# Keys from raw rows with the norm inside their own norm, and TensorE stages of the small work in batches

## The chip, the cores and the metric

The kernel runs on one core of one Trainium2 chip. The metric is the device time of one execution in microseconds (us). A core has TensorE (matrix products, PE in the rows, with its weight loads as PEld), VectorE (DVE), ScalarE (ACT), GpSimd (POOL), and SyncE (SP), which here issues all DMAs.

## What is computed

Two layers of a hybrid trunk over 528 tokens (16 learned ones in front of 512), 1024 wide. Each layer norms its input, projects it once, and feeds two token mixers side by side: a state-space scan over chunks of 128 tokens, and attention over a window of 128 tokens with 16 always visible ones and a sink per head. Both are projected down, gated, added, projected out, and a squared-ReLU feed-forward follows. Cut to what matters here:

```python
for l in range(DEPTH):
    xn = rms_norm(h, norm1_g[l])
    proj = xn @ w_in[l]
    z, xbc, dt_raw, q, k, v, gate_logits = jnp.split(proj, split_at, axis=-1)
    y_ssd = ssd_mixer(z, xbc, dt_raw, ...)
    y_attn = sliding_window_attention(q, k, v, q_norm_g[l], k_norm_g[l], sinks[l])
    g_ssd, g_attn = jnp.split(jax.nn.sigmoid(gate_logits + b_gate[l]), 2, axis=-1)
    merged = g_ssd * (y_ssd @ w_ssd_down[l]) + g_attn * (y_attn @ w_attn_down[l])
    h = h + merged @ w_o[l]
    hn = rms_norm(h, norm2_g[l])
    h = h + jnp.square(jax.nn.relu(hn @ w_mlp_up[l])) @ w_mlp_down[l]

# in the attention, before the scores
q = rotary(rms_norm(q, q_norm_g), pos)
k = rotary(rms_norm(k, k_norm_g), pos)
```

## The kernel before

**Large products.** Activations lie with channels on partitions and tokens along the free axis, eight rows of 128 channels. Every weight matrix is cut into tiles of 1024 x 128. Each float32 operand is split into a high part and a low part that TensorE takes in one pass, so that one product of 1024 x 128 by a span of tokens is 24 matmuls: high by high, high by low and low by high for eight rows. `dense` (line 537) runs one weight tile over its spans of tokens, two of 264 in layer 0 and one of 512 in most of layer 1, and has the result taken out of its PSUM bank. Its argument `by_row` takes the activation rows in the order in which they are made. The order of the tiles is fixed in `layer_order` (line 55): v, two tiles of keys, eight of queries, then eight groups for the scan (six tiles each), with the gates between and behind them, then the down projections and the feed-forward.

**Small work.** The work between the large products (norms, rotary, attention, scan chunks, their tails, the splitting of weights) is written as Python generators. Each `yield` names what the next stage needs: `ps` or `bank` is a PSUM bank, `pe` is TensorE without a new bank, `data`, `after` and `if` are conditions, others are slots of small rings (`po`, the output bank of attention, has one). They stand in six queues, `w, post, misc, tail, chunk, attn`, in that order of preference, with 2, 6, 5, 2, 3 and 3 tasks alive in each.

**The planner.** `Flow` (line 124) keeps a clock for every engine while the program is written out, with costs of its own for each operation; a large product costs n / 2.4 ns, 110 ns for 264 columns. The order that it makes is the order of each engine's instructions. After every second large product `dense` calls `tick` (line 263), which may start stages whose needs are met by TensorE's planned clock: up to 12, but it returns as soon as one of them has moved TensorE's clock, and does nothing while DVE or ScalarE is more than 3500 ns ahead of TensorE. Banks for small work must leave two spare (`SPARED`). Where the program cannot go on without a task it calls `wait_any`, `finish`, `force` or `until`, which run stages with no large products between.

**The start of a layer.** For each row of the input there are the scaled rows `hg` (input times gain, split into high and low parts) and the squares, summed on DVE. The v products (with dt's columns) read `hg` and are scaled by the inverse root afterwards. At `k == KD - 3` (line 871, row 5 of 8) the sums of squares are put on TensorE as twenty one-column matmuls (`rms_tok`, line 606); POOL takes the power, and ten small matmuls spread it over the partitions (`bcast_tok`). Nine tasks `normal_row` (line 759) then make the normed rows `hn` from the input in place, high part by ScalarE, low part by DVE or POOL. The first key tile reads `hn` with `by_row`, so its products follow the rows as they are made. `rope_tile` (line 922) takes a tile of keys or queries out, swaps halves by four DMAs, multiplies by the rotary tables on POOL and DVE, and sums the squares per head on TensorE (ten matmuls of two columns, kept in `rqk`). `head_rms` (line 979) makes the inverse roots. `keys` (line 994) applies them to the keys; for the queries they enter the scores. Two `rope` slots allow two such tiles at a time.

**Attention.** `attention` (line 1040) is one block of 128 queries and four heads: two stages of scores with two banks each, maximum and exponentials, and one to three pieces in which probabilities are transposed, split and multiplied by v. The down projection of attention (`ad`) reads all of it, split by `attn_split` (line 1485).

Of the kernel before, what the change touches and what calls it, by code (L numbers as in the profile page):

```python
# [9 lines left out]
F32 = mybir.dt.float32  # L10
# [3 lines left out]
ALU = mybir.AluOpType  # L14
# [3 lines left out]
P = 128  # L18
D = 1024
KD = D // P  # L20
# [60 lines left out]
class Ring:  # L81


    def __init__(self, n):
        self.free = [0.0] * n
# [38 lines left out]
class Flow:  # L124
# [11 lines left out]
    SPARED = 2  # L136
    WSPARE = 1200.0
    SPARE = 400.0
    WIDTH = dict(w=2, post=6, misc=5, tail=2, chunk=3, attn=3)
    ORDER = ("w", "post", "misc", "tail", "chunk", "attn")  # L140

    def __init__(self, tc):
        self.tc = tc
        self.t = dict.fromkeys(("pe", "v", "s", "g", "sp", "dge", "dma"), 0.0)
        self.prev = {}
        self.rings, self.queues = {}, {}
        self.written, self.read = {}, {}
        self.end = 0.0
        self.last = 0.0
        self.port = {"v": [], "g": []}  # L150


# [108 lines left out]
        return max(self.t["v"], self.t["s"]) - self.t["pe"] > self.AHEAD  # L261

    def tick(self):
        for _ in range(12):
            if self.busy():
                return
            now = self.t["pe"]
            calm = max(self.t["v"], self.t["s"]) - now < self.CALM
            for t, q in self.active():
                if (calm or q is not self.queues["attn"]) and t.at(self) <= now:  # L270
                    self.step(t, q)
                    break
            else:
                return
            if self.t["pe"] > now:
                return

    def wait_any(self):

# [75 lines left out]
def hybrid_trunk_kernel(ctx: ExitStack, tc: tile.TileContext, h0, params, consts, rope, wdt, w, out,  # L355
# [7 lines left out]
    sm = ctx.enter_context(tc.tile_pool(name="sm", bufs=2))  # L363
# [4 lines left out]
    V = Engine(F, "v", nc.vector)  # L368
# [11 lines left out]
    for k in F.ORDER:  # L380
        F.queue(k, F.WIDTH[k])

# [19 lines left out]
    def C(name, rows=P):  # L402
        a, b = CCOL[name]
        return cst[:rows, a:b]
# [31 lines left out]
    def tt_any(out, a, b, op, spare=None):  # L436

        n = Engine.size(out)
        eng = G if max(F.t["g"], F.t["pe"]) + n * 2.09 + 125.0 < max(F.t["v"], F.t["pe"]) + n / 0.96 + (F.SPARE if spare is None else spare) else V
        if eng is V or n < 512:  # L440
# [96 lines left out]
    def dense(spans, tile_, act, evac, after=None, hold=False, by_row=None, late=None, more=(), keep=False):  # L537

        parts = [(tile_, act)] + list(more)
        steps = [(x, k) for ks in (range(KD - 2), range(KD - 2, KD)) for x in range(3) for k in ks]
        late = [late] if late else []
        if by_row:
            steps = [(0, 0)] + [z for k in range(1, KD) for z in ((0, k), (1, k - 1))] + [(1, KD - 1)]
            steps += [(2, k) for k in range(KD)]

        def place():
            if held and F.rings["ps"].at(F.SPARED + 2) == INF:
                leave()  # L550
            return Slot("ps")

        def product(p, ps, a, b, i):
            x, k = steps[i]
            last = p == len(parts) - 1
            if late and last and k >= KD - 2:
                late.pop()()
            whi, wlo = wt[parts[p][0]].slot.parts
            act = parts[p][1]
            mm(ps.t[:, :b - a], (wlo if x == 2 else whi)[:, k, :], (act.lo if x == 1 else act.hi)(k)[:, a:b],  # L560
               start=(p == 0 and i == 0), stop=(last and i == len(steps) - 1))
            if i % 2:
                F.tick()
                if held and all(t.done for t in first):
                    leave()

        def ready(n, ps):
            a, b = spans[n]

            def out_():  # L570
                F.end = 0.0
                evac(ps.t[:, :b - a], a, b, *([ps] if keep else ()))
                if not keep:
                    ps.free()
                if after and n == len(spans) - 1:
                    after()
            held.append(out_)
            if not hold or all(t.done for t in first):
                leave()

        to = []
        if by_row:
            F.finish(wt[tile_])
            to = [place() for _ in spans]
            for i, (x, k) in enumerate(steps):
                if x < 2:
                    F.force(by_row[k + x:k + x + 1])
                for n, (a, b) in enumerate(spans):
                    product(0, to[n], a, b, i)
            wt[tile_].slot.free()  # L590
            for n in range(len(spans)):
                ready(n, to[n])
            return
        for p, (t, _) in enumerate(parts):
            F.finish(wt[t])
            for n, (a, b) in enumerate(spans):
                if p == 0:
                    to.append(place())
                for i in range(len(steps)):
                    product(p, to[n], a, b, i)  # L600
                if n == len(spans) - 1:
                    wt[t].slot.free()
                if p == len(parts) - 1:
                    ready(n, to[n])
# [34 lines left out]
    nrm = {}  # L639
# [61 lines left out]
    hg = Split("hg", KD)  # L701
# [23 lines left out]
    for l in range(depth):  # L725
# [31 lines left out]
        hn = Split("hn", KD)  # L757
# [16 lines left out]
        normal = [F.put("post", normal_row(k)) for k in range(KD + 1)]  # L774
        tables_t = F.put("misc", tables())
# [92 lines left out]

        for k in range(KD + 1):
            F.force(made[k:k + 1])  # L870
            if k == KD - 3:

                F.force(made)
                while not nrm["summed"]:
                    F.step(norm_t[0], F.queues["misc"])
            if k < KD:
                v_row(k, 0, start=k == 0)
            if k:
                v_row(k - 1, 1)
# [20 lines left out]
        for c in range(5):  # L900
            ps = banks[c]
# [17 lines left out]
        kr, kn = kn_u[:, 0:2, :], kn_u[:, 2:4, :]  # L919
        rqk = lay.tile([P, 5, 20], F32, name="rqk", tag="rqk")  # L920

        def rope_tile(kind, spans, m, dst, c_lo):
            slot = Slot("rope")
            j = slot.j
            qx, sq = au[:, j, :T], au[:, 2 + j, :T]
            cosg, sing = table[kind]
            lo = spans[0][0]
            here = []

            def evac(ps, a, b):  # L930
                S.copy(qx[:, a:b], ps)

            def swap():
                here.append(1)

            dense(spans, (l, kind, m), hn, evac, after=swap, by_row=normal if kind == "k" and m == 0 else None)

            def rest():
                yield {"if": lambda: here, "sq": 1}

                t1 = Slot("sq", "t1")
                for o in range(0, P, 32):
                    i = o ^ 32
                    F.dma(t1.t[o:o + 32, lo:T], qx[i:i + 32, lo:T])
                S.activation(out=sq[:, lo:T], in_=qx[:, lo:T], func=AF.Square)
                yield {"after": [tables_t]}
                for x, y in ((lo, 264), (264, T)):
                    G.tensor_tensor(out=dst[:, x:y], in0=qx[:, x:y], in1=cosg[:, x:y], op=ALU.mult)
                yield {"data": lambda: [t1.t[:, lo:T]]}
                tt_any(t1.t[:, lo:T], t1.t[:, lo:T], sing[:, lo:T], ALU.mult)  # L950
                yield {"ps": 1}
                ps = Slot("ps")
                for c in range(c_lo, 5):
                    t0 = CHUNKS[c][0]
                    mm(ps.t[:, 2 * c:2 * c + 2], sq[:, t0:t0 + P], C("blk"))
                slot.free()
                yield

                col = 16 + 2 * m if kind == "k" else 2 * m
                f, e = (1.0 / 64.0, EPS) if kind == "k" else (1.0, 64.0 * EPS)  # L960
                V.tensor_scalar(out=rqk[:, c_lo:, col:col + 2], in0=ps.t[:, 2 * c_lo:10].rearrange("p (c x) -> p c x", x=2),
                                scalar1=f, scalar2=e, op0=ALU.mult, op1=ALU.add)
                ps.free()
                V.tensor_tensor(out=dst[:, lo:T], in0=dst[:, lo:T], in1=t1.t[:, lo:T], op=ALU.add)
                t1.free()
            return F.put("misc", rest())
# [12 lines left out]
        def head_rms(tasks, c0_, h0_, h1_):  # L979

            yield {"after": tasks, "raw": 1}
            tmp = Slot("raw", "rqs")
            t = [tmp.t[:, o:o + 100].rearrange("p (c h) -> p c h", c=5)[:, c0_:, h0_:h1_] for o in (0, 100)]
            v = rqk[:, c0_:, h0_:h1_]
            rsqrt(v, t)
            V.tensor_copy(out=v, in_=t[1])
            tmp.free()

        kt = [rope_tile("k", ALL, m, kr[:, m, :T], 0) for m in range(2)]
# [603 lines left out]
        hg = Split("hg", KD)  # L1593
# [68 lines left out]
        if not last:  # L1662
            hg = hg2
# [106 lines left out]
```

## Time and profile before

| | |
|---|---|
| time, median of 3 runs | 2383.31 us (2380.02 to 2384.53) |
| the profiled execution | 2383.62 us |
| its span, first to last instruction | 2381.5 us |
| mean granted clock of TensorE | 0.991 |
| TensorE busy | 2344.6 us, 98% |
| DVE, ScalarE, POOL busy | 1167.9, 1027.6, 1328.7 us |
| DMA, mean | 108 GB/s |

A row of the timeline gives the start, the time until the last end, the engine, the line, the operation with its tiles, the shapes and a count of merged instructions; in brackets stands idle time before it and what ended it. A matmul's recorded time overlaps that of the next one, so the pace is read from one start to the next. Line 431 is the helper for all matmuls, 434 that for transposes, 348 the wrapper for all other engines, so groups are told apart by their tiles: `hnh` and `hnl` are the parts of the normed rows, `hgh` and `hgl` of the raw scaled rows, `whi` and `wlo` of a weight tile.

### The profile page before, as it was taken

How to read it: one execution, taken by the hardware profiler on the slowest of the kernel's cores; microseconds unless marked ns; L12 is line 12 of the kernel's file. 1: busy time of each engine (PE TensorE's matmuls, PEld its weight loads, DVE VectorE, ACT ScalarE, POOL GpSimd, SP SyncE). 2: the span in 40 equal slices, each digit the busy share in tenths (PEclk: the TensorE clock that was granted, in tenths of full speed). 3: DMA queues.
4: the chain of work that ended last, by engine and by line, in shares of the span. 5: the costliest groups of instructions: out<-in, count | busy, mean ns of one | idle time of the engine just before them, and what ended most of it. 6: DMA issues, size and time to landing. Idle time of an engine off the chain costs nothing.

```text
span 2381.5 us, 41784 instructions
## 1 busy us (share of the span) xinstructions
PE 2344.6 (98%) x16038; PEld 2144.2 (90%) x16038; DVE 1167.9 (49%) x2499; ACT 1027.6 (43%) x2007; POOL 1328.7 (56%) x1751
## 2 busy tenths in 40 slices
PE   7999999999999999999999999999999999999999
PEld 7999999999999999999998888989988788888887
DVE  5577788877412332122146867877773124222121
ACT  5365666555422233232244556656553223333221
POOL 4554555665655555455546554456855655555554
PEclk8999999999999999999999999999999999999999
DMA  4223333443453322222242233334444433222222
GB/s 145 90 86 99 90 100 101 113 102 102 122 184 112 135 81 89 93 94 89 92 153 83 72 115 107 102 98 112 115 121 133 169 117 132 90 96 97 98 91 104
DMA packets 133589, 257.42 MB, mean 108 GB/s; under 512 B 16470, under 2 KB 66318, under 8 KB 133390
## 3 DMA queue, kind: packets, MB, share of 16 engines
q1 hardware_dynamic: 133390, 254.75, 33.9%
q8 instruction: 127, 2.08, 0.3%
q14 instruction: 72, 0.59, 0.1%
HBM read 232.03 MB, written 17.33 MB: 105 GB/s over the span
## 4 chain that ended last, share of the span: by engine, by line
PE 90%; DVE 4%; DMA 2%; ACT 1%; POOL 1%; issue 1%; SPq 0%; POOLq 0%; ACTq 0%; DVEq 0%
PE ps L431 87%; PE ps L434 2%; DMA gm<-ac_dram 2%; DVE at L348 1%; DVE rqs L348 0%; ACT gm L348 0%; DVE xb L348 0%; DVE ar L348 0%; POOL wlo L348 0%; DVE xh L348 0%; DVE h L348 0%; DVE raw L348 0%; ACT whi L348 0%; DVE gm L348 0%; DVE es L348 0%
## 5 line engine op out<-in xcount | busy, mean ns | idle before, releaser
L348 POOL TENSOR_TENSOR wlo<-wraw,whi 128x256 fp32r<-128x256 f32 x1272 | 981.9, 804 | 777.3 <-ACT whi L348 754.3
L348 ACT CAST whi<-wraw 128x1024 fp32r<-128x1024 f32 x340 | 355.5, 1046 | 730.5 <-PE ps L431 698.6
L431 PE MATMUL ps<-hnl,whi 128*128 128x266 f32 (+2 forms) x2048 | 400.7, 311 | 1.7 <-POOL hnl L348 1.5
L431 PE MATMUL ps<-hnh,whi 128*128 128x266 f32 (+2 forms) x2048 | 398.2, 310 | 1.0 <-DVE vm L348 0.6
L431 PE MATMUL ps<-hnh,wlo 128*128 128x266 f32 (+2 forms) x2048 | 393.7, 310 | 0.0
L431 PEld LDWEIGHTS ps<-hnl,whi 128*128 128x128 f32 x2048 | 306.7, 191 | 16.6 <-POOL hnl L348 3.4
L431 PEld LDWEIGHTS ps<-hnh,wlo 128*128 128x128 f32 x2048 | 306.3, 191 | 14.0 <-issue 0.2
L431 PEld LDWEIGHTS ps<-hnh,whi 128*128 128x128 f32 x2048 | 305.1, 190 | 13.8 <-PE ps L431 0.8
L348 DVE SCALAR_TENSOR_TENSOR h<-ps,h 128x264 f32<-128x264 f32 (+1 forms) x120 | 62.2, 518 | 324.3 <-PE ps L431 324.3
L431 PE MATMUL ps<-hgl,whi 128*128 128x264 f32 (+1 forms) x768 | 154.0, 322 | 0.4 <-DVE hgl L348 0.4
L431 PE MATMUL ps<-hgh,wlo 128*128 128x264 f32 (+1 forms) x768 | 153.4, 321 | 0.0
L431 PE MATMUL ps<-hgh,whi 128*128 128x264 f32 (+1 forms) x768 | 153.3, 321 | 0.0
L431 PE MATMUL ps<-hidl,whi 128*128 128x264 f32 (+1 forms) x768 | 152.7, 320 | 0.0
L431 PE MATMUL ps<-hidh,wlo 128*128 128x264 f32 (+1 forms) x768 | 152.6, 320 | 0.0
L431 PE MATMUL ps<-hidh,whi 128*128 128x264 f32 (+1 forms) x768 | 152.5, 320 | 0.0
L348 DVE SCALAR_TENSOR_TENSOR tmp<-ps,rbc 128x264 f32<-128x264 f32 (+1 forms) x96 | 49.5, 515 | 179.0 <-PE ps L431 170.2
L431 PE MATMUL ps<-y,whi 128*128 128x264 f32 (+1 forms) x768 | 137.0, 320 | 0.0
L431 PEld LDWEIGHTS ps<-hgl,whi 128*128 128x128 f32 x768 | 119.3, 189 | 11.5 <-DVE hgl L348 0.6
L431 PEld LDWEIGHTS ps<-hgh,whi 128*128 128x128 f32 x768 | 119.4, 189 | 11.2
L431 PEld LDWEIGHTS ps<-hgh,wlo 128*128 128x128 f32 x768 | 119.1, 189 | 11.0
L431 PEld LDWEIGHTS ps<-hidh,wlo 128*128 128x128 f32 x768 | 118.7, 188 | 11.1
L431 PEld LDWEIGHTS ps<-hidl,whi 128*128 128x128 f32 x768 | 118.7, 188 | 11.0
(213 smaller groups left out, 3892.0 us busy)
## 6 DMA issues: line engine op xcount, KB each, us to landing
wraw<-w_dram SPq DMA_DIRECT2D x344, 512.0 KB, 3.2
gm<-ac_dram SPq DMA_DIRECT2D x64, 256.0 KB, 5.0
et<-ac_dram SPq DMA_DIRECT2D x128, 64.0 KB, 4.6
t<-au SPq DMA_DIRECT2D x48, 66.0 KB, 2.0
h<-h_dram SPq DMA_DIRECT2D x8, 264.0 KB, 5.7
at<-rope_dram SPq DMA_DIRECT2D x4, 528.0 KB, 4.1
y_dram<-xb SPq DMA_DIRECT2D x4, 528.0 KB
yr<-y_dram SPq DMA_DIRECT2D x8, 264.0 KB, 3.1
```

Source lines behind the costliest of these rows:

```text
L348: inst = fn(*a, **k)
L431: F.run("pe", cost, [o], [lhsT, rhs], PE.matmul(out=o, lhsT=lhsT, rhs=rhs, start=start, stop=stop))
L434: F.run("pe", 108.0 if in_.shape[1] > 64 else 60.0, [o], [in_], PE.transpose(out=o, in_=in_, identity=C("ident", k)[:, :k]))
```

## The change

The planner gets a field `GAP` of 3600 ns. In `tick`, stages that need TensorE or a bank are passed over unless that much of TensorE's planned time has gone by since the end of the last batch; other stages go on. In an open tick up to 24 stages may start, and it no longer returns after the first one on TensorE. The key tiles take `hg` in place of `hn`. Their scale is then missing the inverse root r of the token's norm: the head sums are multiplied by r squared (`r2`) before the small constant is added, and the inverse roots of the keys by r. `by_row` goes to the first query tile. The rest of the key work waits for all `normal_row` tasks, since its output lies on the buffer of the input rows. In layer 0 the sums of squares move from row 5 to behind row 7.

```diff
+    GAP = 3600.0
+        self.batch = 0.0

     def tick(self):
-        for _ in range(12):
+        begin = self.t["pe"]
+        open_ = begin - self.batch >= self.GAP
+        for _ in range(24):
             if self.busy():
-                return
+                break
             now = self.t["pe"]
             calm = max(self.t["v"], self.t["s"]) - now < self.CALM
             for t, q in self.active():
+                if not open_ and any(k in ("pe", "ps", "bank") for k in t.needs):
+                    continue
                 if (calm or q is not self.queues["attn"]) and t.at(self) <= now:
                     self.step(t, q)
                     break
             else:
-                return
-            if self.t["pe"] > now:
-                return
+                break
+        if self.t["pe"] > begin:
+            self.batch = self.t["pe"]

-            if k == KD - 3:
+            if k == (KD - 3 if l else KD):

+        r1 = nrm["rt"]
+        r2 = sm.tile([P, 5], F32, name="rt2", tag="rt2")
+        V.tensor_tensor(out=r2, in0=r1, in1=r1, op=ALU.mult)

-            dense(spans, (l, kind, m), hn, evac, after=swap, by_row=normal if kind == "k" and m == 0 else None)
+            dense(spans, (l, kind, m), hg if kind == "k" else hn, evac, after=swap,
+                  by_row=normal if kind == "q" and m == 0 else None)

-                yield {"after": [tables_t]}
+                yield {"after": [tables_t] + (normal if kind == "k" else [])}

-                V.tensor_scalar(out=rqk[:, c_lo:, col:col + 2], in0=ps.t[:, 2 * c_lo:10].rearrange("p (c x) -> p c x", x=2),
-                                scalar1=f, scalar2=e, op0=ALU.mult, op1=ALU.add)
+                o = rqk[:, c_lo:, col:col + 2]
+                x = ps.t[:, 2 * c_lo:10].rearrange("p (c x) -> p c x", x=2)
+                if kind == "k":
+                    V.scalar_tensor_tensor(out=o, in0=x, scalar=f, in1=r2[:, c_lo:, None].broadcast_to([P, 5 - c_lo, 2]),
+                                           op0=ALU.mult, op1=ALU.mult)
+                    V.tensor_scalar(out=o, in0=o, scalar1=e, scalar2=None, op0=ALU.add)
+                else:
+                    V.tensor_scalar(out=o, in0=x, scalar1=f, scalar2=e, op0=ALU.mult, op1=ALU.add)

-            V.tensor_copy(out=v, in_=t[1])
+            if h0_ == 16:
+                V.tensor_tensor(out=v, in0=t[1], in1=r1[:, c0_:, None].broadcast_to([P, 5 - c0_, h1_ - h0_]), op=ALU.mult)
+            else:
+                V.tensor_copy(out=v, in_=t[1])
```

## Rows read from the trace of the kernel before

**Rows 1.** The page, part 1: busy us, share of span, instructions.
```profile
PE 2344.6 (98%) x16038; PEld 2144.2 (90%) x16038; DVE 1167.9 (49%) x2499; ACT 1027.6 (43%) x2007; POOL 1328.7 (56%) x1751
```
**Rows 2.** The page, part 4: the chain that ended last, by line.
```profile
PE ps L431 87%; PE ps L434 2%; DMA gm<-ac_dram 2%; DVE at L348 1%; DVE rqs L348 0%; ACT gm L348 0%; DVE xb L348 0%; DVE ar L348 0%; POOL wlo L348 0%; DVE xh L348 0%; DVE h L348 0%; DVE raw L348 0%; ACT whi L348 0%; DVE gm L348 0%; DVE es L3
```
**Rows 3.** Timeline of PE near 602 us (start, us, engine, operation, count).
```profile
602.00 0.89 PE L431 MATMUL ps<-hnh,wlo 128*128 128x264 f32 x6
602.73 0.41 PE L431 MATMUL ps<-hnh,whi 128*128 128x264 f32 x2
...
603.94 0.49 PE L434 MATMUL ps<-cst,xb 128*128 128x128 f32 x3
604.27 0.39 PE L431 MATMUL ps<-xb 128*128 128x128 f32 x2
604.41 0.49 PE L431 MATMUL ps<-hnh,whi 128*128 128x264 f32 x2
604.74 0.91 PE L431 MATMUL ps<-hnl,whi 128*128 128x264 f32 x6
```
**Rows 4.** Timeline of PE: sums of squares of layer 0, next v products.
```profile
18.41 3.40 PE L431 MATMUL ps<-cst,sq 128*128 128x1 f32 x20 [1.35 <-DVE sq L348]
...
21.67 1.55 PE L431 MATMUL ps<-wvh,hgh 128*128 128x288 f32 x5
```
**Rows 5.** Timeline of DVE and POOL: the root of these sums.
```profile
21.85 0.17 DVE L348 TENSOR_SCALAR rt<-ps 128x5 f32<-128x5 f32 x1 [1.31 <-PE ps L431]
...
22.09 1.18 POOL L348 TENSOR_TENSOR rt<-rt,cst 128x5 f32<-128x5 f32 x1 [11.43 <-DVE na L348]
```
**Rows 6.** Timeline of PE: the two key tiles of layer 0.
```profile
35.19 0.65 PE L431 MATMUL ps<-hnh,whi 128*128 128x264 f32 x4
...
43.24 1.11 PE L431 MATMUL ps<-hnl,whi 128*128 128x264 f32 x2 [0.44 <-POOL hnl L348]
...
47.32 0.90 PE L431 MATMUL ps<-hnh,whi 128*128 128x264 f32 x6
...
53.29 1.06 PE L431 MATMUL ps<-cst,adt 128*32 128x128 f32 x8
```
**Rows 7.** Timeline of PE: the first key tile of layer 1.
```profile
1255.32 0.60 PE L431 MATMUL ps<-hnh,whi 128*128 128x264 f32 x3 [0.59 <-DVE vm L348]
```
**Rows 8.** PE's waits (us, times, longest); uses of `ar` (ns min/median/max).
```profile
PE ps L431 <- DVE ar L348: 5.8, 11, 1.6
PE ps L431 <- POOL rx L348: 3.5, 3, 1.7
...
L348 DVE TENSOR_TENSOR ar<-ps,ar x92: 205/681/693, 120.2 to 1641.1; 128x512 fp32r<-128x512 f32 x56, 32x512 fp32r<-32x512 f32 x32, 16x64 fp32r<-16x64 f32 x4
```
**Rows 9.** Stretches: length, busy (count) of PE, PEld, DVE, ACT, POOL, clock, DMA, GB/s.
```profile
19.60:26.40 6.80, 6.80 (x31) 6.80 (x31) 1.19 (x4) 2.26 (x5) 1.18 (x1) 0.50 0.43 157
...
40.00:46.90 6.90, 6.06 (x24) 4.99 (x23) 6.28 (x17) 2.29 (x7) 3.70 (x6) 0.51 0.23 77
...
84.40:91.20 6.80, 6.80 (x32) 6.80 (x33) 6.45 (x9) 2.58 (x4) 3.21 (x6) 0.50 0.37 117
...
118.50:660.00 541.50, 533.60 (x4343) 508.48 (x4343) 400.88 (x964) 313.86 (x756) 300.07 (x395) 1.00 0.36 102
...
1241.50:1245.00 3.50, 3.50 (x17) 3.50 (x17) 0.17 (x1) 0.79 (x3) 1.17 (x1) 0.51 0.37 139
```
**Rows 10.** Timeline of PE: scores begin, attention ends, `ad` begins, per layer.
```profile
108.23 0.28 PE L431 MATMUL ps<-k2h,q 128*128 128x256 f32 x1
...
447.89 0.63 PE L431 MATMUL ps<-ar,vt 128*128 128x512 f32 x2
...
665.87 0.90 PE L431 MATMUL ps<-ah,whi 128*128 128x264 f32 x6
...
1642.96 0.62 PE L431 MATMUL ps<-ar,vt 128*128 128x512 f32 x2
...
1841.31 1.55 PE L431 MATMUL ps<-ah,whi 128*128 128x512 f32 x6
```

## The prediction

> **What bounds the kernel now.** I read the busy table first: TensorE (PE in the rows) is busy 2344.6 of 2381.5 us [rows 1], so only some 37 us are open idle time, and the reader should expect a change of order to be worth a per cent or two at most. The chain of waits says the same: 87% of it is the large and small matmuls of one helper line [rows 2]. So the time is the sum of what TensorE has to stream, plus its waits, plus the stretches at the lower clock. The other engines matter only where TensorE waits for them or where they set when a buffer comes free.
>
> The large products run at a plain pace: six of 264 columns take 602.00 to 602.73, 0.122 us each [rows 3]. A small matmul between them takes about 0.11 us (603.94 to 604.27 for three transposes). Is a change-over from large to small and back dear? From 603.94 to 604.74 there are five small and two large matmuls in 0.80 us [rows 3]; five at 0.11 and two at 0.122 make 0.79. So a change-over costs about 0.01 us, and **fewer, longer interruptions gain next to nothing by themselves**. What batching can win is waits and clock. Both have prices in the trace: the waits list [rows 8], and four of the stretches at 0.50 to 0.51 of the full clock [rows 9], where a large product takes twice its time, so that a stretch of 6.8 us loses 3.4 and one of 3.4 loses 1.7.
>
> The profiled execution took 2383.62 us, of which 2381.5 are the span; the median of the three runs is 2383.31, so the sum below may be set against 2383.6.
>
> **The change part by part: the start of layer 0.** Before, the sums of squares stand behind the v products of row 4. TensorE waits 1.35 us for the last one, the twenty one-column matmuls end at 21.67, and from 19.6 to 26.4 the clock is at half, 1.2 GHz [rows 4, 9]. After, they stand behind the products of row 7: six more groups of five at 0.13 us (288 columns by the pace above), 4 us, which cover the wait. I take back the wait, 1.35, and the half clock, 3.4 us. New is that only five v products (0.7 us) then stand between the sums and the broadcast that needs their root: DVE takes 0.17 us and POOL 1.18 us for it, until 23.27, and with a hop it is some 1.75 us after the sums [rows 5]. So about 1.1 us of wait appears; it would be nothing if the planner's tick runs the sums a row earlier. Sum: 1.35 + 3.4 - 1.1 = 3.7 us gained, bounds 2 and 5.
>
> Then the first key tile. Before, it reads the normed rows as they are made: from 35.19 to 47.32, 12.1 us, with waits such as 0.44 us for a row from POOL, and the clock at half from 40.0 to 46.9 [rows 6, 9]. The second tile takes 47.32 to 53.29, 6.0 us. With raw rows both inputs are there long before, since the v products have just read them; the first tile then takes 48 x 0.122 = 5.9 us and 6.2 us come back. The wait for rows moves to the first query tile, which starts after two key tiles, 11.7 us later. Its rows were complete by about 43.2 before [rows 6]; after, the key tiles end near 35.2 - 3.7 + 11.7 = 43.2, and the ten tiny matmuls of the first key tile's head sums go ahead of the queries as they did before. The rows start no later, because the v products ahead of the root run at full clock. So I charge 0.5 us, bounds 0 and 2.5. The rest of the key work waits for all the normed rows (its output overlies them); that wait sits in the planner's queue, and behind it on POOL stand the rotary products of the keys and the low parts of weights. The head sums themselves need only ScalarE's square, so TensorE is not held. The added scaling is some six DVE operations on 5 to 10 numbers per partition, 0.17 us each by the nearest row [rows 5], beside TensorE's products: nothing on the path, 1 us if the cover were gone. The squared norm is right by algebra and moves no DMA; the four swaps of each key tile leave SP in the same order behind its copy, some 6 us earlier. Layer 0 in sum: 3.7 + 6.2 - 0.5 = **9.4 us**, bounds 5 and 11.5.
>
> Layer 1 keeps its place of the sums, so its half clock from 1241.5 stays. Its first key tile waits only 0.59 us [rows 7], which goes: **0.6 us**, bounds 0 and 1.
>
> **The batches.** A stage that needs TensorE may now begin only when 3600 ns of planned products have passed since the last batch: at the planner's 110 ns that is 34 large products (it looks after every second one), 34 x 0.122 = 4.15 us plus the batch itself. Steps on DVE, ScalarE and POOL go on in between. A stage that became ready inside the gap has then been ready for up to 4 us, so the plan's small errors no longer show as waits. The waits that belong to such stages are led by 5.8 us for the split probabilities and 3.5 for the key factors [rows 8]; with six smaller ones of that list they are about 18 us. A stage that becomes ready just before its batch still waits, and inside a batch several stages follow each other without products between them. I take half, **9 us**, bounds 2 and 15. For the clock: the stretch from 84.4 [rows 9] follows a wait for the key factors and loses 3.4 us. I take that back, **3 us**, bounds -8 (longer runs of tiny matmuls lower the clock elsewhere) and 8.
>
> The price is latency. Each chain now moves at most one TensorE stage per batch. Attention is the longest: in layer 0 there are 20 tasks (five blocks, four heads of keys), four with one piece, four with two and twelve with three; only one may hold the output bank, and one with n pieces passes n+1 stages there, so 4x2 + 4x3 + 12x4 = 68 stages in a row. Before, scores start at 108.2 and the last value product stands at 447.9: 340 us, 5.0 us per stage. The products that need all of it start at 665.9 [rows 10]. From 108.2 to there stand some 3140 large products, 92 batches of 34, 6.05 us each with the small work. At one stage per batch attention ends at 108 + 68 x 6.05 = 520 us; at 1.35 batches per stage it ends just at 666. Layer 1 has 60 stages and 198 us of slack [rows 10], so it bears about 1.45. Between two stages lie a copy, a subtraction of 0.68 us [rows 8] and the queue of DVE, which is 74% busy from 118.5 to 660 [rows 9], so most steps fit one gap and some need two; I take 1.25, which costs nothing. The last group's chunks must be through at the same point and also pass one gap per stage: I charge **2 us** for both layers as an allowance, bounds 0 and 15 (three batches of some 5 us). The feed-forward half has almost no such stages and stays.
>
> Sum: 2383.6 - 9.4 - 0.6 - 9 - 3 + 2 = 2363.6, say **2363 us**, 0.9% faster.
>
> **The rivals.** First, the keys gain, the batches do not: waits move from single stages to the heads of batches and the clock is as before. Then 2383.6 - 10 = 2373, still faster. For it: TensorE's waits are already short and spread. Against: they come where plan and chip differ by a few tenths, and a gap of 4 us is longer.
>
> Second, on the slow side: **attention is starved**. There are eight banks; a span of large products holds one and often its predecessor's, two are kept spare, the output holds one, and a score stage wants two at once. When a batch gives two to chunks first, scores must wait for the next, since no bank comes free inside a batch. By this mechanism a stage costs 1.6 batches in layer 0: of 92 batches 109 are wanted, 17 are missing, some 11 stages run with no products above them at about 2.5 us each (copy, subtraction, hops, the wait for the next), and the splitting of eight rows of about 1 us follows uncovered: 27 + 8 = 35 us, so 2398. It decides at 1.35 batches per stage. For it: DVE's load, and that attention comes last in the order of the queues. Against: before, the pace was 5.0 us where 558 / 68 = 8.2 are allowed. The Trainium skill ("Trainium Kernel Development and Optimization", Best Practices) names exhausted PSUM as a cause of regular gaps; no run here shows it for this kernel.
>
> Third, **the clock**. It fell at 1241.5 although TensorE was busy in all of that stretch [rows 9], right behind twenty one-column matmuls. Batches put such sums, ten at a time, beside others. Seven more stretches of 6.8 us would take 24 us: 2387. Against: from 118.5 to 660 the clock was 1.00 throughout [rows 9]. The Trainium skill ("TensorE: Matmul & The Clock Gate", HAM oscillation) ties the fall to waits between bursts; by that rule alone bunching would only help, but the trace shows a fall without idle time.
>
> Last, that the change does not do what it says: the query tile inherits the whole wait for the rows and the drop of the clock with it, and nothing is won at the start: 2373.
>
> **How the numbers follow.** The forecast has 0.53, the first rival 0.15, starved attention 0.18, the clock 0.09, the inherited wait 0.05. The forecast's own range is 2350 to 2374. To leave out no more than 2 in 10 the range goes from 2350 to 2397, which takes in most of the starved case. Faster by over 0.2% (4.8 us, about what a measurement of this kernel can tell from no change) is the forecast, nearly all of the first and last rivals: 0.71. Within 0.2% come most of the clock's case and mild starvation: 0.12. Slower: 0.17.
>
> **What would show each step.** The first key tile some 6 us long and starting near 31.5 us, no half clock from 19.6 to 26.4 nor from 40 to 47, and no row waits in the first query tile; runs of small matmuls some 34 products apart; less waiting on the split probabilities and key factors; the last value product of layer 0 between 500 and 650 us, and no idle TensorE before the products that read attention. The prediction is wrong if that point shows attention stages with gaps, if half-clock stretches multiply between 118 and 660, or if the first query tile waits as the first key tile did.

## The result and the profile after

The changed kernel takes 2352.59 us (median; 2351.39 to 2355.22) against 2383.92 for the kernel before on the same chip: a ratio of 0.9877 with a 95% interval of 0.9865 to 0.9889. The forecast was 2363. The profiled execution took 2351.39 us, its span is 2349.5.

The page of the changed kernel, part 1 (busy us, share, count), answers to [rows 1]:

```profile
PE 2322.6 (99%) x16038; PEld 2129.6 (91%) x16038; DVE 1186.7 (51%) x2511; ACT 1027.7 (44%) x2007; POOL 1327.6 (57%) x1733
```

TensorE runs the same 16038 matmuls and is busy 22 us less: what was saved is mostly time in which it counted as busy. Lines 439, 442 and 356 are here what 431, 434 and 348 were before; the numbers differ from version to version. TensorE's waits (total us, times, longest) answer to [rows 8]:

```profile
PE ps L439 <- ACT wvh L356: 9.5, 1, 9.5
PE ps L439 <- DVE q L356: 5.2, 2, 4.6
PE ps L439 <- DVE ar L356: 2.2, 3, 0.8
...
PE ps L439 <- POOL rx L356: 0.5, 1, 0.5
```

The first line is the wait for the first weights, which every version has. The split probabilities `ar` fell from 5.8 to 2.2 us, the key factors `rx` from 3.5 to 0.5. A new one of 4.6 us stands before the first scores. Four stretches (columns as in [rows 9]):

```profile
19.60:26.40 6.80, 6.06 (x49) 5.80 (x49) 2.16 (x6) 2.53 (x5) 1.18 (x1) 1.00 0.46 157
40.00:46.90 6.90, 6.90 (x60) 6.90 (x59) 6.11 (x11) 3.65 (x9) 6.62 (x9) 1.00 0.59 179
...
94.40:101.20 6.80, 4.59 (x21) 4.62 (x22) 3.95 (x19) 1.97 (x4) 2.06 (x4) 0.50 0.04 10
...
835.10:841.90 6.80, 6.80 (x33) 6.80 (x33) 0.17 (x1) 0.32 (x1) 1.18 (x1) 0.50 0.22 77
```

The clock is whole where [rows 9] had it at half (19.6, 40.0), and the last two lines are all the half clock that is left between the first rise of the clock and the last matmul: 13.7 us, where the kernel before had 41 in eight stretches.

The timeline of TensorE at the start of layer 0 answers to [rows 4, 6]:

```profile
20.90 2.29 PE L439 MATMUL ps<-cst,sq 128*128 128x1 f32 x20
23.05 0.91 PE L439 MATMUL ps<-wvh,hgl 128*128 128x288 f32 x5
24.70 1.48 PE L439 MATMUL ps<-cst,rt 16*128 16x16 f32 x10 [0.74 <-POOL rt L356]
25.93 5.49 PE L439 MATMUL ps<-wvl,hgh 128*128 128x288 f32 x40
31.26 0.89 PE L439 MATMUL ps<-hgh,whi 128*128 128x264 f32 x6
...
33.70 0.51 PE L439 MATMUL ps<-hgh,wlo 128*128 128x264 f32 x2 [0.34 <-POOL wlo L356]
...
37.66 0.90 PE L439 MATMUL ps<-hgh,whi 128*128 128x264 f32 x6
...
44.58 0.73 PE L439 MATMUL ps<-hnh,whi 128*128 128x264 f32 x4
```

The sums have no wait, the broadcast of the root waits 0.74 us, the first key tile takes 6.4 us from 31.26, and the first query tile, which begins at 44.58, runs through the normed rows without a wait. Attention, for [rows 10]: the last value product of layer 0 and the first product that reads attention:

```profile
577.87 0.70 PE L439 MATMUL ps<-ar,vt 128*128 128x512 f32 x2
...
642.10 0.89 PE L439 MATMUL ps<-ah,whi 128*128 128x264 f32 x6
```

**Where the time went.** Every large product has the same number in both kernels, so the time between two of them can be compared. "Waits" is TensorE's idle time there, "clock" half of the time in which it was busy in half-clock stretches (a wait in such a stretch counts as a wait alone), "rest" what is left; gains in us.

| Large products | before | after | gain | waits | clock | rest |
|---|---|---|---|---|---|---|
| 0 to 120, v | 25.99 | 21.80 | 4.2 | 0.6 | 3.4 | 0.2 |
| to 216, two key tiles | 20.23 | 13.31 | 6.9 | 1.7 | 3.0 | 2.2 |
| to 600, queries, first scores | 76.55 | 74.07 | 2.5 | -1.2 | 4.5 | -0.9 |
| to 3672, rest of attention's half | 533.90 | 523.45 | 10.5 | 6.5 | 0 | 3.9 |
| to 8280, feed-forward half | 567.49 | 569.01 | -1.5 | 0 | -1.7 | 0.2 |
| to 11500, the same half of layer 1 | 726.42 | 716.72 | 9.7 | 2.6 | 5.1 | 2.0 |
| to the end | 417.52 | 417.51 | 0 | 0 | 0 | 0 |

In sum 32 us: 10 of waits, 14 of clock, 8 that fall under neither.

### The profile page after: what moved, and what is told of

Read it like the earlier page. It is cut to its first block, busy times and chain, and to the rows that moved or that the text cites. A ratio compares the mean times of both kernels' runs of the same rounds, so it can differ in the third digit from the quotient of the medians.

```text
span 2349.5 us, 41761 instructions
## 1 busy us (share of the span) xinstructions
PE 2322.6 (99%) x16038; PEld 2129.6 (91%) x16038; DVE 1186.7 (51%) x2511; ACT 1027.7 (44%) x2007; POOL 1327.6 (57%) x1733
## 4 chain that ended last, share of the span: by engine, by line
PE 92%; DVE 4%; ACT 1%; POOL 1%; issue 1%; DMA 1%; SPq 0%; ACTq 0%; DVEq 0%; POOLq 0%
PE ps L439 90%; PE ps L442 3%; DVE rqs L356 1%; DVE at L356 1%; DVE xh L356 0%; POOL wlo L356 0%; DVE xb L356 0%; DMA gm<-ac_dram 0%; ACT gm L356 0%; ACT whi L356 0%; DVE raw L356 0%; DVE ar L356 0%; DVE gm L356 0%; DVE qa L356 0%; SPq L232 0%
## 5 line engine op out<-in xcount | busy, mean ns | idle before, releaser
L439 PE MATMUL ps<-hnh,whi 128*128 128x266 f32 (+2 forms) x1984 | 371.7, 305 | 0.0
L439 PE MATMUL ps<-hnl,whi 128*128 128x266 f32 (+2 forms) x1984 | 369.5, 305 | 0.0
L439 PE MATMUL ps<-hnh,wlo 128*128 128x266 f32 (+2 forms) x1984 | 365.6, 304 | 0.0
L439 PEld LDWEIGHTS ps<-hnl,whi 128*128 128x128 f32 x1984 | 293.0, 189 | 13.4
L439 PEld LDWEIGHTS ps<-hnh,wlo 128*128 128x128 f32 x1984 | 291.6, 189 | 13.2
L439 PEld LDWEIGHTS ps<-hnh,whi 128*128 128x128 f32 x1984 | 292.0, 189 | 12.6 <-issue 0.3
L439 PE MATMUL ps<-hgh,wlo 128*128 128x264 f32 (+1 forms) x832 | 165.0, 320 | 0.3 <-POOL wlo L356 0.3
L439 PE MATMUL ps<-hgl,whi 128*128 128x264 f32 (+1 forms) x832 | 164.5, 319 | 0.4 <-DVE hgl L356 0.4
L439 PE MATMUL ps<-hgh,whi 128*128 128x264 f32 (+1 forms) x832 | 164.1, 319 | 0.0
L439 PEld LDWEIGHTS ps<-hgh,wlo 128*128 128x128 f32 x832 | 128.6, 190 | 11.5 <-POOL wlo L356 0.5
L439 PEld LDWEIGHTS ps<-hidl,whi 128*128 128x128 f32 x768 | 118.8, 188 | 11.1
L439 PEld LDWEIGHTS ps<-hidh,wlo 128*128 128x128 f32 x768 | 118.7, 188 | 11.1
```

Of the source, the lines that this page charges most:

```text
L439: F.run("pe", cost, [o], [lhsT, rhs], PE.matmul(out=o, lhsT=lhsT, rhs=rhs, start=start, stop=stop))
```

## The experiments

Two theories stood against each other for the batches. **Time in hand**: a stage that begins some microseconds after the plan calls it ready doesn't show the plan's errors as waits, and no half clock follows them. **Change-overs**: each turn from large to small matmuls costs by itself, and fewer turns gain. The kernel before plans a stage on TensorE 0.1 us behind the step before it (`LATP = 100.0`), so the gap between batches is one way to give a stage time, a larger `LATP` is another.

All twelve in one table with the kernels before and after, each ratio against executions of the kernel before in the same round (medians 2381.96 to 2383.92 us). The balance is that of the profiled execution, from the first matmul to the last; the first 3 to 6 us, ahead of the clock's first rise, are at half clock too and stand in the rest. "Turns" is the count of runs of small matmuls, "last value" the end of the last value product of layer 0.

| Kernel | median us | ratio to before, 95% | turns | waits | clock | rest | last value |
|---|---|---|---|---|---|---|---|
| before | 2383.92 | | 484 | 23.9 | 20.1 | 2324.5 | 448 |
| after | 2352.59 | 0.9865 to 0.9889 | 220 | 13.7 | 5.7 | 2316.8 | 579 |
| keys_only | 2378.68 | 0.9970 to 0.9989 | 489 | 22.0 | 20.9 | 2321.7 | 472 |
| batches_3200 | 2370.10 | 0.9921 to 0.9958 | 230 | 18.5 | 16.1 | 2321.1 | 582 |
| both_3200 | 2360.75 | 0.9892 to 0.9922 | 227 | 16.5 | 9.1 | 2317.8 | 581 |
| spread_3200 | 2376.50 | 0.9968 to 0.9987 | 485 | 20.9 | 15.1 | 2319.8 | 645 |
| gap_0 | 2401.79 | 1.0056 to 1.0100 | 355 | 38.1 | 25.6 | 2323.0 | 429 |
| gap_1800 | 2372.27 | 0.9941 to 0.9979 | 291 | 24.0 | 11.8 | 2319.3 | 506 |
| margin | 2362.91 | 0.9895 to 0.9934 | 482 | 16.8 | 16.8 | 2316.1 | 603 |
| sums_early | 2356.88 | 0.9872 to 0.9906 | 221 | 14.3 | 11.1 | 2317.1 | 582 |
| margin_1000 | 2350.34 | 0.9851 to 0.9884 | 483 | 8.4 | 10.0 | 2318.2 | 518 |
| b1800_l1500 | 2353.73 | 0.9864 to 0.9893 | 298 | 11.0 | 12.7 | 2316.5 | 562 |
| cost_550 | 2391.26 | 1.0022 to 1.0048 | 211 | 39.9 | 19.7 | 2318.4 | 655 |
| margin_1000_cost | 2373.69 | 0.9948 to 0.9978 | 490 | 26.5 | 14.3 | 2318.7 | 524 |

The rest lies between 2316 and 2323 us for all the changed versions, and doesn't go with the turns: the lowest, margin, has 482, the highest, gap_0, 355. What tells them apart is mostly the waits and the clock, which together run from 18 to 64 us.

**keys_only**: the change with the old tick.

```diff
-        for _ in range(24):
+        for _ in range(12):
...
-                if not open_ and any(k in ("pe", "ps", "bank") for k in t.needs):
-                    continue
...
+            if self.t["pe"] > now:
+                return
```

> Keys from raw rows and the later sums, with the planner's old tick (one TensorE stage per tick, no gap). Theory, margin: the keys gain 10 us at the start of layer 0 and 0.6 in layer 1, the rest of the gain belongs to the batches: 2373 us, bounds 2368 and 2377; the first key tile takes 6 us, the half-clock stretches at 19.6 and 40 us are gone, those further on remain in number. Rival, all from the keys: the batches only look as if they gained, because the keys shift the rest: 2355 us.

It took 2378.68 us, less than half of the gain that was expected. The start did gain: the first query tile ends 11.0 us earlier, counted from the first matmul. But from product 8280 to 11500 it lost 8.6 us (735.00 against 726.42), with waits of 12.0 where there were 8.3 and a clock loss of 10.2 where there were 5.1. TensorE's order there is another one than in the kernel before, again with stages 0.1 us behind the plan; that the earlier start throws the order, and that the order makes the waits, is my reading and was not tested. And of the half clock at the start, which was to be gone, 6.8 us stand at 24.6.

**batches_3200 and both_3200**: the new tick with a gap of 3200 ns on the kernel before (old keys, old place of the sums), and the whole change with that gap.

```diff
-    GAP = 3600.0
+    GAP = 3200.0
```

> The kernel before with the new tick and a gap of 3200 ns of planned products, keys from normed rows. Theory, margin: the batches gain what the keys do not, some 20 us: 2363 us, bounds 2358 and 2370, with PE's waits on split probabilities below 3 us and fewer half-clock stretches after 60 us. Rival, all from the keys: 2384. The start of layer 0 stays as before, with a first key tile of 12 us.

> The changed kernel with a gap of 3200 instead of 3600 ns, the control for the two runs that use 3200. All theories: 2353 us, bounds 2349 and 2357; some 240 runs of small matmuls.

2370.10 and 2360.75: the batches give some 13 us without the new keys, the keys another 9 with the batches. The second lies above what was expected, the first just past its upper bound: with 400 ns less between batches the gain is smaller (both_3200 against the changed kernel: 0.9907 and 0.9877, with intervals that don't meet).

**gap_0 and gap_1800**: the whole change with gaps of 0 and of 1800 ns; the first edit is

```diff
-    GAP = 3600.0
+    GAP = 0.0
```

> The changed kernel with a gap of 0: a tick may set up to 24 stages at once, but none is held back. Theory, margin: without the gap no stage has time in hand, so the waits on late inputs come back as in the kernel before: 2371 us, bounds 2366 and 2376. Rival, many stages per tick are what counts: 2355.

> The changed kernel with half the gap, 1800 ns. Theory, margin: half the time in hand covers more than half of the small errors of the plan: 2358 us, bounds 2353 and 2364. Rival, change-overs: the gain of the batches goes with the number of runs of small matmuls, which rises to some 330: 2362.

Both theories missed both runs. gap_1800, at 2372.27, lies 8 us above the upper bound of the first and 10 above the figure of the second, with 291 turns. gap_0, at 2401.79, is slower than the kernel before, though it has 355 turns where that has 484. An open tick at gap 0 starts all stages that are ready, each as soon as the plan allows, with no large products between. Its waits, first four lines, and one of them in the timeline:

```profile
PE ps L439 <- POOL xdd L356: 10.8, 5, 3.0
PE ps L439 <- DVE ar L356: 9.8, 12, 4.5
PE ps L439 <- ACT wvh L356: 9.2, 1, 9.2
PE ps L439 <- DVE q L356: 5.0, 2, 4.5
```

```profile
315.33 0.50 PE L439 MATMUL ps<-ar,vm 128*128 128x512 f32 x1 [0.71 <-DVE ar L356]
```

`ar` alone is 9.8 us in 12 waits, [rows 8] had 5.8 in 11. So grouping without distance did harm here. Its waits are 38.1 us in sum; with the gap they fall to 24.0 (1800), 16.5 (3200) and 13.7 us (3600), and the time with them. Fewer turns gained nothing.

**spread_3200**: gap 3200, but the stages that a batch would hold start one in each tick, with two large products between.

```diff
-        open_ = begin - self.batch >= self.GAP
+        open_ = self.left or begin - self.batch >= self.GAP
...
+            if self.t["pe"] > begin:
+                break
...
         if self.t["pe"] > begin:
+            self.left = True
             self.batch = self.t["pe"]
+        else:
+            self.left = False
```

> As the control with a gap of 3200, but the stages of a batch are set one per tick with two large products between, until none is ready; so stages have waited as long as in the control, while the small work interrupts the products about twice as often (some 450 runs of small matmuls). Theory, margin: a change-over costs 0.01 us, so within 4 us of the control. Rival, change-overs: bunching itself is the gain, some 0.08 us for each of 220 more interruptions: 15 to 20 us slower than the control.

It took 2376.50, 16 us more than both_3200, which is the number of the change-over theory, and by time alone that theory would stand. The balance says otherwise: with 485 turns in place of 227 its rest is 2.0 us larger, 0.008 us for each turn more, where 16 us would be 0.06. The loss has a place. From product 3672 to 4056, the first that read attention, it took 62.9 us where both_3200 took 46.7:

```profile
644.40 0.63 PE L444 MATMUL ps<-ar,vt 128*128 128x512 f32 x2
...
647.09 0.41 PE L444 MATMUL ps<-ah,whi 128*128 128x264 f32 x2
649.29 0.92 PE L444 MATMUL ps<-ah,whi 128*128 128x264 f32 x2 [1.79 <-ACT ah L361]
652.17 1.12 PE L444 MATMUL ps<-ah,whi 128*128 128x264 f32 x2 [1.96 <-ACT ah L361]
...
657.54 0.81 PE L444 MATMUL ps<-al,whi 128*128 128x264 f32 x2 [2.91 <-POOL al L361]
...
661.32 1.17 PE L444 MATMUL ps<-cst,zs 128*128 128x1 f32 x4 [1.66 <-DVE zs L361]
```

```profile
650.40:667.50 17.10, 10.35 (x39) 8.96 (x40) 10.27 (x17) 7.92 (x16) 14.20 (x22) 0.50 0.43 141
```

The last value product stands at 644.40, the products that read it begin at 647.09. TensorE waits 8.9 us there for the split of the rows and the last chunks, and the clock is at half for 17.1 us. That is the starved attention of the prediction's second rival: 68 stages in 541 us are 8.0 us each. Outside this place spread_3200 is some 4 us faster than both_3200 in the two profiles; its profile is the fastest of its ten executions, 5.6 us below their median, so a part of the 16 us has no place.

**margin**: keys_only with 2.0 us in hand for each stage on TensorE, no batches.

```diff
-    LATP = 100.0
+    LATP = 2000.0
```

> Keys from raw rows with the planner's old tick, and LATP raised from 100 to 2000 ns: a TensorE stage counts as ready 2 us after its inputs by the plan, and there is no gap and no batch. Theory, margin: time in hand is what gains, so most of the batches' gain comes without batches: 2358 us, bounds 2353 and 2365, with some 450 runs of small matmuls. Rival, change-overs: no batches, no gain over keys alone: 2373.

2362.91, within what the theory allowed, with 482 turns. Of the 26 us between keys_only and the changed kernel it brings 16 with no batch at all. And it loses some that it need not: two rows of its timeline among the products that read attention, where the tails of the last chunks are late.

```profile
641.90 0.58 PE L433 MATMUL ps<-cst,zs 128*128 128x1 f32 x4 [0.91 <-DVE zs L350]
646.85 1.32 PE L433 MATMUL ps<-cst,rg 128*128 128x128 f32 x4 [4.37 <-POOL rg L350]
```

With a half clock behind them this place costs 9.3 us (56.0 against 46.7). Another 6.9 go in layer 1, where products 8280 to 11500 take 724.21 us and in margin_1000, the next run, 717.32. Two microseconds for each stage were too much here.

**margin_1000**: the same with 1.0 us.

> The new keys without batches, each stage on TensorE planned 1.0 us behind the step before it, where 0.1 us was planned and 2.0 us in the run margin. The theory, that time in hand is what the batches give: most single waits of the kernel without it were under 1.7 us, so 1.0 us catches the larger part, and attention is no longer late at the products that read it, where 2.0 us cost 5.3 us of waits and 3.4 of clock: 2362 us (2356 to 2368), some 480 runs of small matmuls. The rival, that only distances of several microseconds between stages help: 2372.

2350.34 us (2348.41 to 2355.34), a ratio of 0.9868: below what was expected, and not to be told from the changed kernel, with 483 turns and no batches. Its waits, the first three lines:

```profile
PE ps L433 <- ACT wvh L350: 9.3, 1, 9.3
PE ps L433 <- DVE mx L350: 2.8, 2, 1.8
PE ps L433 <- ACT whi L350: 0.8, 1, 0.8
```

`ar` and `rx` are gone. So one number in the planner gives the whole gain without a batch, and attention ends at 518 rather than 579. That time in hand is also what the batches give is the reading that fits the four gaps, whose waits fall as the gap grows. It is not proof: each version is one order, and two below have time in hand and are 23 and 39 us slower.

**b1800_l1500**: batches 1800 ns apart and 1.5 us in hand.

```diff
-    LATP = 100.0
+    LATP = 1500.0
...
-    GAP = 3600.0
+    GAP = 1800.0
```

> The changed kernel with batches 1800 ns apart (2372.27 us at 0.1 us in hand) and each stage on TensorE planned 1.5 us behind the step before it. If time in hand decides: 2357 us (2351 to 2363), with some 290 runs of small matmuls as before. If the distance between batches decides: 2372, as without it.

2353.73, as expected: the gap that gave 2372.27 gives all of the gain once the stages have time. With time in hand, the distance between batches no longer counts.

**sums_early**: the changed kernel with the sums of layer 0 back at their old place.

```diff
-            if k == (KD - 3 if l else KD):
+            if k == KD - 3:
```

> The changed kernel with the sums of squares of layer 0 back behind row 4. Theory: the wait of 1.35 us and the half clock behind it return and the exposed root goes, 3.7 us worse: 2356.5 us, bounds 2355 and 2358. Rival, the key tiles now give the norm room and the place of the sums no longer matters: 2352.6.

2356.88, 4.3 us more than the changed kernel, but the intervals of the two overlap (0.9872 to 0.9906, 0.9865 to 0.9889), so the times alone don't prove it. In the profiles the v products take 4.2 us longer, 3.4 of it half clock. That half clock turns out to be a matter of chance, as the last two sections show.

**cost_550 and margin_1000_cost**: the wait of 4.58 us before the first scores. In the timeline of the changed kernel, TensorE first, then DVE:

```profile
77.15 1.56 PE L439 MATMUL ps<-cst,rx 128*64 128x128 f32 x18
...
91.15 0.88 PE L439 MATMUL ps<-hnh,wlo 128*128 128x264 f32 x6
96.61 0.55 PE L439 MATMUL ps<-k2h,q 128*128 128x256 f32 x1 [4.58 <-DVE q L356]
```

```profile
87.69 0.72 DVE L356 TENSOR_SCALAR rqs<-rqk 128x40 int32<-128x40 int32 x1
...
89.13 0.68 DVE L356 TENSOR_TENSOR rqs<-rqk,rqs 128x40 f32<-128x40 f32 x1
...
95.77 0.68 DVE L356 TENSOR_TENSOR q<-qa,q 64x512 fp32r<-64x512 f32 x1
```

Twelve operations on 40 numbers per partition take 8 us, and the low part of the queries, which the scores need, stands behind them. The edit tells the planner that they are long:

```diff
+            F.t["v"] += 11 * 550.0
+            F.end = max(F.end, F.t["v"])
```

> The changed kernel, with one number of its plan changed: the eleven DVE operations on 128x40 numbers that turn the sums of the heads into the roots are planned 0.55 us longer each, since they took 0.66 to 0.74 us in the profile of the changed kernel. The theory: the first scores then are begun later in the order, their wait of 4.58 us at 96.61 us goes, and the half clock from 94.4 to 101.2 us behind it (3.4 us) with it: 2352.6 - 8 = 2344.6 us (2340 to 2350). The rival: the order after that point is thrown again and as much is lost elsewhere: 2352.6, give or take 4.

> margin_1000 with the eleven DVE operations of the roots planned 0.55 us longer each. The theory: waits of the first scores on the low part of the queries go in both layers (7.1 us and a half clock in layer 1 of the run margin): 6 to 9 us below margin_1000, about 2354 us (2348 to 2362) without any batches. The rival: the same time as margin_1000.

Both theories failed in both runs: 2391.26 and 2373.69, 39 us and 23 us slower than without the edit. Three rows of TensorE and one of DVE, of cost_550:

```profile
101.23 1.56 PE L439 MATMUL ps<-cst,rx 128*64 128x128 f32 x18
109.78 0.58 PE L439 MATMUL ps<-k2h,q 128*128 128x256 f32 x1 [6.98 <-DVE q L356]
...
114.05 0.58 PE L439 MATMUL ps<-k2h,q 128*128 128x256 f32 x1 [3.06 <-POOL q L356]
```

```profile
98.80 0.20 DVE L356 TENSOR_TENSOR rqs<-rqk,rqs 128x40 f32<-128x40 f32 x1
```

The planner now holds DVE busy for 6 us in which it isn't, and holds back other stages for it. The second set of key factors comes at 101.23, where the changed kernel has it at 77.15, and the first scores follow with no large product between: two waits of 10 us in sum. Attention begins 13 us later and ends at 655, so that the products that read it wait 12.0 us more. And the twelve operations themselves took 3.3 us here, most of them some 0.2 us each: the price that the edit wrote into the plan was that of another order. In margin_1000_cost 12 of the 23 us go before product 600 (82.91 from product 216 on, against 70.99). Whether a change of the order alone, without a false price, would win the 4.58 us back was not tried.

Longer gaps than 3600, to drive attention into starvation by batches, were not tried either.

## Why the prediction was right, and where its sizes were off

**Sums of squares, forecast 3.7.** 4.2 came back up to product 120: the clock 3.4, the wait 1.35, and 0.74 of new wait for the root where 1.1 had been charged. But the step that took back the half clock is right only by chance. In the 11 versions with the sums behind row 7 TensorE's order is the same up to the first query tile; four (after, both_3200, gap_0, margin_1000_cost) keep the full clock behind the sums, seven lose it from a moment between 23.5 and 25.7 us. There this stretch takes 24.5 (gap_1800) to 26.2 us (b1800_l1500), against 25.99 before: a gain of 1.5 to nothing. The term should have been 0 to 4, and that it came out at its size is luck.

**First key tile, forecast 6.2.** The two tiles together gained 6.9: 1.7 of waits, 3.0 of clock, 2.2 of rest. The first takes 6.4 us (31.26 to 37.66) instead of 12.1, 0.34 of it a wait for a low part of weights that the sum hadn't. The waits for rows went as forecast; the 12.1 holds a half clock that one profile showed. In batches_3200, with the keys still from normed rows, the clock was whole there and the same tile took 9.3 us, so that without it some 3 of the 6.2 are left.

**Query tile, forecast 0.5 lost.** Nothing was lost: rows wait nowhere in it. The rival by which it would inherit the wait is out.

**Layer 1's first key tile, forecast 0.6.** The wait of 0.59 is gone.

**Batches' waits, forecast 9.** From product 216 on, attention's halves had 19.6 us of waits before and 11.7 after: 8, of which 0.6 is layer 1's key tile. Of what is left 4.58 are the one new wait. The mechanism was right as far as the runs go: margin_1000, with time in hand and no batches, has 7.0 us there.

**Clock, forecast 3.** Beyond the start it gave 7.9: 4.5 before product 600, 5.1 in layer 1, less 1.7 in the feed-forward half. That some half clock goes was right, the size and the place were not: the sum counted the stretch at 84.4 of [rows 9], and that one stayed (94.4 in the changed kernel, where it begins in the new wait), while those at 57.1, 115.1, 1241.5 and 1303, of which it counted none, went, and the one in the feed-forward half grew from 3.4 us at 859.2 to 6.8 at 835.1. The one at 1241.5 was to stay, since the sums of layer 1 keep their place. Twelve of the 14 versions have it, four of them with TensorE's order of the changed kernel from product 8280 to 8400; that it went is luck as well.

**Latency, forecast 2 lost.** No cost: between 3672 and 4056, the first products that read attention, both kernels take 46.7 us. Attention took 7.1 us per stage (482 us for 68), 1.28 batches (87 in that time) with a median of 32 large products between them, where 1.25 and 34 had been taken. The rival of starved attention did not come in this kernel, but its mechanism is real: spread_3200 and cost_550, at 8.0 us per stage, pay 16 and 19 us at the products that read attention; cost_550 has 92 batches for its 68 stages, the 1.35 that the prediction named. Its place was right, and the changed kernel stayed 1 us per stage below the point from which it decides.

**What had no term.** The rest gave 8 us, 5 of it behind product 216. Between the two profiles 32 us were gained, where the sum had 20. Of the 12 between, 5 are this rest, 5 the clock, 2 the latency and 2 the start, less 2 by which the waits fell short. The rest isn't change-overs: from product 216 to 11500, without the feed-forward half, it is 1300.3 us with 220 turns and 1301.5 with 483 (margin_1000), under 0.01 us for each turn, which is the prediction's figure. In the kernel before it is 1305.3, in keys_only 1304.4. Over all versions it runs from 1298.0 (margin) to 1306.2 (gap_0) and follows neither the turns nor the waits: cost_550, with the most waits, has 1298.7. What it is made of stays open.

**The first rival**, keys gain and batches don't, forecast 2373: keys_only came to 2378.68, with most of the gain of the start lost again in layer 1. The keys alone gave 4.5 us, batches of 3200 alone 13.1, both together 22.5, each against the kernel before in the same round; with the intervals of the three it can't be told whether the halves add.

## What to carry to other kernels

Where a planner writes the order, give each stage on the busy engine about as much time in hand as the plan's errors are long (here 1 us, of waits that were mostly under 1.7), and not so much that the longest chains of stages pass their slack (here 2 us did). Count that chain first: stages times distance against the time until it is read. By these runs batches are one way to get this time, not a gain in themselves, and an edit upstream can be judged only with the waits that its new order brings further down. A half-clock stretch is priced from more than one profile.

## What the runs showed of the hardware

**The same order can lose the clock or keep it.** The two rows are the same time, in which TensorE runs the same part of the same order, from the changed kernel and from margin_1000 (columns as in [rows 9]):

```profile
23.90:30.70 6.80, 6.06 (x47) 5.97 (x47) 4.29 (x10) 2.80 (x6) 4.00 (x7) 1.00 0.06 22
```

```profile
23.90:30.70 6.80, 6.36 (x28) 5.97 (x27) 3.42 (x9) 1.90 (x3) 2.88 (x4) 0.50 0.05 17
```

In the four executions that kept it, the full clock had been granted from 12.1 to 12.5 us on; in the seven that lost it, from 13.2 to 15.5. So 3.4 us at the start hang on a moment that TensorE's order doesn't set, and a stretch seen once in one profile is no sure term of a sum. Executions of one kernel differ too: the kernel before ran eight times beside gap_0, with mean granted clocks of 0.991 to 0.996 and times of 2386.36 to 2376.47 us. The Trainium skill ("TensorE: Matmul & The Clock Gate", What's actually happening) says that the number of slow matmuls at the start changes from run to run of the same kernel; the traces agree, across kernels that begin with the same order (full clock from 12.1 to 15.5 us), and show the same for the fall behind it.

**The clock often falls at tiny matmuls with hardly a wait, and not always.** In the feed-forward half of the changed kernel:

```profile
833.08 0.39 PE L439 MATMUL ps<-hgl,whi 128*128 128x264 f32 x1 [0.39 <-DVE hgl L356]
...
835.36 0.57 PE L439 MATMUL ps<-cst,sq 128*128 128x1 f32 x2
```

Twenty one-column matmuls stand between 833.31 and 835.8, the only wait is 0.39 us, and the clock is at half from 835.1 to 841.9, as in [rows 9] at 1241.5. Each of the 14 versions has three such groups of twenty: at 33 of the 42 the clock fell while they ran or within 1.5 us behind them, at 9 it didn't. In cost_550, with TensorE's order of the changed kernel from product 4056 to 8280, the same group ends at 870.4 us, and behind it:

```profile
870.20:877.00 6.80, 6.80 (x55) 6.63 (x55) 0.60 (x2) 1.43 (x2) 3.45 (x5) 1.00 0.20 71
```

**Short DVE operations cost what runs beside them.** The operation `rqs<-rqk,rqs` on 128x40 took 0.68 us at 89.13 in the changed kernel, where POOL splits weights and multiplies by turns, and 0.20 at 98.80 in cost_550, where POOL had just ended. The Trainium skill ("SBUF — State Buffer", Who interferes with whom) says that a DVE instruction with two inputs in SBUF contends with a GpSimd instruction that reads SBUF; the trace agrees, with DVE operations of 0.65 to 0.74 us beside POOL's of 0.7, and of 0.5 beside POOL's of 0.53. Operations with one input took as long, though: the last of the twelve, a copy, 0.65 us at 95.09 against 0.18 in cost_550, which that sentence doesn't cover.
